# A hybrid decoder layer: wide moving operands and plain float32 in the small products

## The chip, the core and the metric

The kernel runs on one core of a Trainium2 chip. The metric is the device time of one launch in microseconds (us). Five engines work side by side, each through its own instructions in order: TensorE (PE, with its weight loads as PEld), VectorE (DVE), ScalarE (ACT), GpSimd (POOL) and SyncE (SP), which here only issues DMA transfers. Semaphores tell one engine that another has finished. The median of three runs before the change is 497.67 us (496.89 to 497.83).

## What is computed

The input x has 256 tokens of 1024 features. One product with `w_in` gives ten groups of 1024 columns: A_X and A_G (recurrent branch and its gate), S_U and S_V (spatial branch), Q, K and V (attention), G_A, G_S and G_M (a merge gate for each branch). Cut to its core, the reference is:

```python
a_x, a_gate, s_u, s_v, q, k, v, g_a, g_s, g_m = split(x @ w_in)
y_a = rg_lru(causal_dwconv(a_x, conv_w, conv_b), w_r, b_r, w_i, b_i, lam) * gelu(a_gate)
y_s = gelu(s_u) * (tril(w_s[g]) @ layer_norm(gelu(s_v)) + b_s)   # per group g, chunks of 128 tokens
y_m = moba_attention(q, k, v)          # 8 heads of 128; 256 tokens are one causal block
merged = sigmoid(g_a) * y_a + sigmoid(g_s) * y_s + sigmoid(g_m) * y_m
x1 = layer_norm(alpha * x + merged @ w_out)
h_gate, h_up = split(x1 @ w_up)        # 3072 columns each
out = layer_norm(alpha * x1 + (gelu(causal_dwconv(h_gate)) * h_up) @ w_down)
```

`rg_lru` has two block-diagonal gates, r and i (eight blocks of 128 x 128 each), and a scan over the tokens.

## The kernel before

**Three passes.** A large product is made of float32r operands: each operand is split into a rounded part, hi, and the rest, lo, and the products hi·hi, hi·lo and lo·hi are summed (`passes`). ScalarE copies a block into hi, and VectorE subtracts hi from it into lo (`split`, L64 to L66). This holds for weights and for activations.

**Chunks.** The weights come in 80 chunks of 128 x 2048 (1 MB). Forty belong to `w_in` (four of 256 columns for each group, with all eight k-tiles), four to `w_out`, 36 to the feed-forward part. `load` brings a chunk as two DMAs into two raw buffers of 1024 columns (five such buffers), `prep` splits each half. Chunks 1 to 3 come in pieces of 512, chunk 0 in eight pieces that hold a k-tile of x and one of the weights (256 columns each, 256 KB). The hi and lo parts have four buffers each, so chunk n + 4 takes the place of chunk n and can be split only when the products with chunk n are done. Loads run three chunks ahead (`LOOK`).

**Two layouts.** Feature-major (`fm_pe`, L213): the weights are stationary, the 256 tokens move, the result has features on the partitions. Token-major (`tm_mm`, L230): the activations are stationary, 256 weight columns move, the result has tokens on the partitions. S_V and V are token-major before, the other eight groups feature-major. Either way a chunk is 48 matmuls of 256 moving columns. `w_out` and `w_down` (`row_mm`, L621 to L630) move 512 columns, 24 matmuls to a chunk.

**Small products.** The mixers (`mix_step`, L367) are plain float32, 128 moving columns. The r and i gates (`ri_step`, L406), the scores of the second query tile (`score_step`, L508) and most of attention times v (`pv_step`, L562) are three-pass products of 256 columns, for which xc, `wrg`, q, k, v and the probabilities are split too. Transposes (L542, L668) are matmuls with an identity.

**The merge.** `gs_step` takes a quarter of the features at a time: sigmoid, product with the spatial branch, two sums, split into mgh and mgl. `wo0_step(c)` needs the quarter c of them.

**Order.** The program is a list of steps. TensorE's instructions stand as the list has them. The other engines' order is made by a scheduler when the kernel is built, except in the layer norm region behind `wo0_step` and in the last steps, where they keep to the list. Each engine runs its row strictly in order. Result banks are two sets of four, psa for projections, psb for the small products; a step must wait until the bank that it takes over has been read. The end of the list up to the first layer norm is q and k, scores, transposes and attention, with the projections G_A and G_S between them to cover the softmax.

Of the kernel before, what the change touches and what calls it, by code (L numbers as in the profile page):

```python
# [46 lines left out]
def trunk_kernel(ctx: ExitStack, tc, xw, x, w_in, wrg, wsT, w_out, w_up, w_down, rows, packed, out):  # L47
# [32 lines left out]
    def load(i):  # L80
        """A chunk in two halves, or, for the first chunks, in parts the arithmetic needn't wait long for"""
        parts = loaded[i] = []
        if i == 0:
            # k-tiles of the activations and of the chunk side by side
            pair = [U(f"xw{h}", (P, 4, 2, S)) for h in range(2)]
            for k in range(KT):
                t = pair[k // 4][:, k % 4 : k % 4 + 1]
                nc.sync.dma_start(t, xw[:, k : k + 1])
                parts.append((t, slice(k * S, (k + 1) * S), slice(k, k + 1)))
            return  # L90
        raw = [raws.tile([P, 1024], F32, name=f"raw{i}{h}", tag="raw") for h in range(2)]
# [992 lines left out]
```

## Time and profile before

| what | value |
|---|---|
| median of the runs (three) | 497.67 us |
| span of the profiled execution, first to last instruction | 495.1 us |
| TensorE busy | 485.0 us (98%) |
| VectorE busy | 337.7 us (68%) |
| ScalarE busy | 271.6 us (55%) |
| moved by DMA | 92.95 MB, 188 GB/s |
| granted TensorE clock, mean | 0.997 |

The span leaves out what the launch needs around the first and last instruction, so it stands 2.6 us under the median; the page gives no time of its own for the profiled execution. A matmul's duration in the trace holds its way through the array, and the next one starts long before it ends: durations of 283 ns stand 120 ns apart. What a stream of matmuls costs is therefore read from start to start. A number in brackets behind a timeline row is the time for which the engine stood before it, with what it waited for.

### The profile page before, as it was taken

The numbers are of one execution on the slowest core, as the hardware profiler recorded it, in microseconds if no ns is written. First come the engines' busy times: TensorE is split into PE (matmuls) and PEld (weight loads), VectorE is DVE, ScalarE is ACT, GpSimd is POOL, SyncE is SP. The second block draws the span as 40 slices with busy tenths as digits, with TensorE's granted clock in tenths as the row PEclk, the third lists the DMA queues.
The fourth block names the chain that finished last, engine by engine and source line by source line (L and its number), as shares of the span: only waits on it lengthen the run. The fifth ranks groups of instructions, "written<-read, shape, count | busy, mean of one in ns | idle before, by whom it ended". The sixth has DMA issues, their size and how long they took to land.

```text
span 495.1 us, 9096 instructions
## 1 busy us (share of the span) xinstructions
PE 485.0 (98%) x3728; PEld 469.7 (95%) x3728; DVE 337.7 (68%) x527; ACT 271.6 (55%) x410; POOL 21.7 (4%) x24
## 2 busy tenths in 40 slices
PE   8999999999999999999999999999999999999993
PEld 7999999999999999999998999999999999999983
DVE  5889896454449978766685987765666556666635
ACT  6746754465489288567451477645544454444431
POOL 1020000000000000000000800000000000000003
PEclk9999999999999999999999999999999999999998
DMA  8996866474523396674452448776555556555002
GB/s 288 341 372 212 283 210 219 129 228 154 169 86 128 114 317 204 206 267 137 162 170 86 133 149 280 246 252 195 190 174 191 184 184 206 171 175 178 31 1 85
DMA packets 27385, 92.95 MB, mean 188 GB/s; under 512 B 3152, under 2 KB 3536, under 8 KB 27344
## 3 DMA queue, kind: packets, MB, share of 16 engines
q1 hardware_dynamic: 27344, 92.37, 55.8%
q8 instruction: 29, 0.48, 0.4%
q14 instruction: 12, 0.10, 0.1%
HBM read 91.31 MB, written 1.05 MB: 187 GB/s over the span
## 4 chain that ended last, share of the span: by engine, by line
issue 47%; PE 41%; DVE 3%; ACT 1%; POOL 1%; ACTq 0%; DVEq 0%; POOLq 0%
PE p_u L223 14%; PE p_d L628 12%; PE p_g L223 12%; PE p_tg L237 2%; PE p_dq L628 1%; POOL rs_sv L195 1%; ACT hi L65 1%; DVE lo L66 0%; DVE va L200 0%; DVE st_m L187 0%; DVE x1Tl L66 0%; POOL rs_m L195 0%; DVE x L676 0%; PE p_x1t L668 0%; PE p_g L802 0%
## 5 line engine op out<-in xcount | busy, mean ns | idle before, releaser
L66 DVE TENSOR_TENSOR lo<-raw,hi 128x1024 fp32r<-128x1024 f32 (+1 forms) x162 | 189.0, 1193 | 81.3 <-ACT hi L65 80.6
L65 ACT CAST hi<-raw 128x1024 fp32r<-128x1024 f32 (+1 forms) x164 | 160.3, 1015 | 111.2 <-PE p_g L223 28.3
L628 PE MATMUL p_d<-hi,act 128*128 128x512 f32 x180 | 55.7, 391 | 0.0
L628 PEld LDWEIGHTS p_d<-hi,act 128*128 128x128 f32 x180 | 33.1, 188 | 6.3
L628 PE MATMUL p_d<-lo,act 128*128 128x512 f32 x90 | 35.0, 389 | 0.0
L319 DVE SCALAR_TENSOR_TENSOR cv<-p_g,par,cv 128x255 f32<-128x255 f32 (+1 forms) x48 | 23.1, 480 | 7.1 <-ACT cv L317 6.3
L223 PE MATMUL p_u<-x1Th,hi 128*128 128x256 f32 x192 | 27.0, 283 | 0.0
L223 PE MATMUL p_u<-x1Th,lo 128*128 128x256 f32 x192 | 27.0, 283 | 0.0
L223 PE MATMUL p_u<-x1Tl,hi 128*128 128x256 f32 x192 | 26.9, 283 | 0.0
L223 PEld LDWEIGHTS p_u<-x1Th,hi 128*128 128x128 f32 x192 | 25.3, 191 | 0.8
L223 PEld LDWEIGHTS p_u<-x1Th,lo 128*128 128x128 f32 x192 | 24.8, 192 | 0.0
L223 PEld LDWEIGHTS p_u<-x1Tl,hi 128*128 128x128 f32 x192 | 24.8, 192 | 0.0
L317 ACT ACTIVATE cv<-p_g,par 128x256 f32<-128x256 f32 x24 | 13.5, 563 | 19.8 <-DVE cv L319 19.8
L760 DVE TENSOR_TENSOR cv<-cv,p_u 128x512 f32<-128x512 f32 x12 | 8.2, 686 | 22.1 <-PE p_u L223 22.1
L223 PE MATMUL p_g<-x1Th,hi 128*128 128x256 f32 x160 | 22.5, 283 | 0.0
L223 PE MATMUL p_g<-x1Tl,hi 128*128 128x256 f32 x160 | 22.5, 283 | 0.0
L223 PE MATMUL p_g<-x1Th,lo 128*128 128x256 f32 x160 | 22.5, 283 | 0.0
L223 PEld LDWEIGHTS p_g<-x1Th,hi 128*128 128x128 f32 x160 | 20.6, 192 | 0.0
L223 PEld LDWEIGHTS p_g<-x1Tl,hi 128*128 128x128 f32 x160 | 20.6, 192 | 0.0
L223 PEld LDWEIGHTS p_g<-x1Th,lo 128*128 128x128 f32 x160 | 20.6, 192 | 0.0
L628 PEld LDWEIGHTS p_d<-lo,act 128*128 128x128 f32 x90 | 16.9, 188 | 3.6
L744 ACT ACTIVATE cv<-cv 128x512 f32<-128x512 f32 x12 | 7.6, 632 | 11.3 <-DVE cv L319 11.3
(241 smaller groups left out, 981.7 us busy)
## 6 DMA issues: line engine op xcount, KB each, us to landing
raw<-in_w_in SPq DMA_DIRECT2D x72, 512.0 KB, 5.1
raw<-in_w_up SPq DMA_DIRECT2D x48, 512.0 KB, 4.5
raw<-in_w_down SPq DMA_DIRECT2D x24, 512.0 KB, 4.7
raw<-in_w_out SPq DMA_DIRECT2D x8, 512.0 KB, 4.0
raw<-in_w_in SPq DMA_DIRECT2D x12, 256.0 KB, 5.4
xw<-in_xw SPq DMA_DIRECT2D x8, 256.0 KB, 4.9
gb<-in_rows SPq DMA_DIRECT2D x2, 512.0 KB, 8.1
rg_raw<-in_wrg SPq DMA_DIRECT2D x2, 512.0 KB, 6.5
```

What stands on the lines that cost most here:

```text
L65: nc.scalar.copy(hi, src)
L66: sub.tensor_sub(lo, src, hi.bitcast(F32))
L195: nc.gpsimd.tensor_tensor(rs, ve, half, op=ALU.pow)
L223: nc.tensor.matmul(dst[:, j, :], w[:, k, j * P : (j + 1) * P], a[:, k, :], start=(n == 0), stop=(n == 3 * KT - 1))
L237: nc.tensor.matmul(dst, a[:, k, tok * P : (tok + 1) * P], w[:, k, :], start=(m == 0 and k == 0), stop=(m == 2 and k == KT - 1))
L317: nc.scalar.activation(dst, src, AF.Identity, bias=pcol(bname, f), scale=w(taps - 1))
L319: nc.vector.scalar_tensor_tensor(dst[:, d:], src[:, : S - d], w(taps - 1 - d), dst[:, d:], op0=ALU.mult, op1=ALU.add)
L628: nc.tensor.matmul(dst, a[:, k0 + k, tok * P : (tok + 1) * P], w[:, k, s], start=(start and n == 0), stop=(stop and n == 6 * len(parts) - 1))
L744: nc.scalar.activation(t, t, AF.Gelu_apprx_tanh)
L760: nc.vector.tensor_mul(t, t, pf["u", c])
```

## The change

Seven of the ten input groups (`WIDE`) become token-major with 512 weight columns moving; a chunk is then 512 columns of four k-tiles, and two chunks make a half group (`wide_step`). A_X, Q and K stay feature-major (`TALL`). The first eight loads hold 256 columns of x and 512 of weights (384 KB). The raw buffers are three of 2048 columns, and from chunk 4 on a chunk is split by one ScalarE and one VectorE instruction of 2048 columns. The r and i gates, all scores, attention times v and the mixers are plain float32, and the splits for them are gone. The mixers' results and the gated branches are now token-major; `gate_step` and `merge_step` turn them into features with 32 transposes. G_A moves up beside the r and i gates, and the halves of G_S stand between the attention steps. In the names of tiles, p_w is a wide step's bank, p_ag and p_z those of the transposes.

```diff
+WIDE = (S_V, S_U, A_G, G_A, G_M, V_, G_S)
+TALL = (A_X, Q_, K_)
...
-    raws = ctx.enter_context(tc.tile_pool(name="raws", bufs=5))
+    raws = ctx.enter_context(tc.tile_pool(name="raws", bufs=3))
...
-    up = ctx.enter_context(tc.tile_pool(name="up", bufs=10))
+    up = ctx.enter_context(tc.tile_pool(name="up", bufs=9))
...
+        if i in (0, 1):
+            for k in range(4 * i, 4 * i + 4):
+                if k % 2 == 0:
+                    pair = U(f"xw{k}", (P, 2, 768))
+                t = pair[:, k % 2, :]
+                nc.sync.dma_start(t, xw[:, k, :])
+                parts.append((t, k))
             return
-        raw = [raws.tile([P, 1024], F32, name=f"raw{i}{h}", tag="raw") for h in range(2)]
+        raw = raws.tile([P, 2048], F32, name=f"raw{i}", tag="raw")
         w = 512 if i < 4 else 1024
         for at in range(0, 2048, w):
-            r = raw[at // 1024][:, at % 1024 : at % 1024 + w]
-            nc.sync.dma_start(r, chunks[i][:, at : at + w])
-            parts.append((r, slice(at, at + w), None))
+            s = slice(at, at + w)
+            nc.sync.dma_start(raw[:, s], chunks[i][:, s])
+            if w == 512:
+                parts.append((raw[:, s], s))
+        if w == 1024:
+            parts.append((raw, slice(0, 2048)))
...
+        for r, s in loaded.pop(i):
+            if i > 1:
                 split(r, hi[:, s], lo[:, s], subs.get(i, nc.vector))
                 continue
-            h, l = (t[:, s].rearrange("p (k m) -> p k m", m=S) for t in (hi, lo))
-            (nc.vector.tensor_copy if k.start == 0 else nc.scalar.copy)(h, r[:, :, 1, :])
-            split(r[:, :, 0, :], xh[:, k, :], xl[:, k, :])
-            nc.vector.tensor_sub(l, r[:, :, 1, :], h.bitcast(F32))
+            k = s
+            h, l = (t[:, (k % 4) * 512 : (k % 4 + 1) * 512] for t in (hi, lo))
+            w = r[:, 256:]
+            (nc.vector.tensor_copy if k == 0 else nc.scalar.copy)(h, w)
+            split(r[:, :256], xh[:, k, :], xl[:, k, :])
+            nc.vector.tensor_sub(l, w, h.bitcast(F32))
...
+    def wide_mm(i, dst, tok, kh, ks, ms=(0, 1, 2)):
+        hi, lo = (t.rearrange("p (k m) -> p k m", k=4) for t in ready[i])
+        pairs = passes(hi, lo, xh, xl)
+        for k in ks:
+            for m in ms:
+                w, a = pairs[m]
+                at = 4 * kh + k
+                nc.tensor.matmul(dst, a[:, at, tok * P : (tok + 1) * P], w[:, k, :],
+                                 start=(m == 0 and at == 0), stop=(m == 2 and at == KT - 1))
+    def wide_step(group, nh, use, khs=(0, 1)):
+        for kh in khs:
+            i = chunk(w_wide[4 * WIDE.index(group) + 2 * nh + kh])
+            def pe(i=i, kh=kh):
+                if kh == 0:
+                    cur["w"] = [psa.tile([P, 512], F32, name=f"p_w{group}{nh}{tok}", tag="ps") for tok in range(2)]
+                if group == S_V and nh == 0:
+                    for k in range(5):
+                        for ks, ms in (((k,), (0,)), ((k - 1,), (1, 2))):
+                            for tok in range(2):
+                                if 0 <= ks[0] < 4:
+                                    wide_mm(i, cur["w"][tok], tok, kh, ks, ms)
+                    return
+                for tok in range(2):
+                    wide_mm(i, cur["w"][tok], tok, kh, range(4))
+            def post():
+                for tok in range(2):
+                    use(tok, nh, cur["w"][tok])
+            step(pe, [i], post if kh else None)
...
     def load_rg():
...
+        rg["f"] = raw = U("rg", (P, 2, KT, P))
+        nc.sync.dma_start(raw.rearrange("p m g j -> p (m g j)"), wrg)
...
+        def pe():
+            cur["pm"] = p = psb.tile([P, 2, 2, P], F32, name=f"p_mix{c}", tag="ps")
             for j in range(2):
...
+                nc.tensor.matmul(p[:, j], ws["f"][:, g, :], va[:, :, g * P : (g + 1) * P], start=True, stop=True)
...
+            for j in range(2):
+                g = 2 * c + j
+                y = gu["f"][:, :, g * P : (g + 1) * P]
+                nc.vector.scalar_tensor_tensor(y, p[:, j], pcol("bs", g), y, op0=ALU.add, op1=ALU.mult)
...
+    def ga_use(tok, nh, p):
+        t = tmp.tile([P, 512], F32, name=f"sga{tok}{nh}", tag="t0")
+        nc.scalar.activation(t, p, AF.Sigmoid)
+        y = ag["f"][:, tok, HALVES[nh]]
+        nc.vector.tensor_mul(y, y, t)
...
             for m in range(2):
-                ops = passes(rg["h"], rg["l"], xc["h"], xc["l"])
-                for n, (w, a) in enumerate(ops):
-                    nc.tensor.matmul(p[:, m, :], w[:, m, g, :], a[:, g, :], start=(n == 0), stop=(n == 2))
+                nc.tensor.matmul(p[:, m, :], rg["f"][:, m, g, :], xc["f"][:, g, :], start=True, stop=True)
...
+            t = tmp.tile([P, 2, S], F32, name=f"i{g}", tag="t0")[:, 0, :]
+            nc.scalar.activation(t, p[:, 1, :], AF.Sigmoid, bias=pcol("bi", g))
+            nc.vector.tensor_mul(xc["f"][:, g, :], xc["f"][:, g, :], t)
...
+        hs["f"] = sq = U("sq")
...
-            nc.vector.tensor_mul(ga["f"][:, g, :], ga["f"][:, g, :], sq[:, g, :])
...
+            qk[which, c] = t = tmp.tile([P, 2, S], F32, name=f"{which}f{c}", tag=f"{which}f")
+            nc.scalar.copy(t, cur["p"])
...
                 cur["s"].append(p)
-                (qh, ql, qf), (kh, kl, kf) = qk["q", c], qk["k", c]
-                nc.tensor.matmul(p[:, :P], qf[:, j, :], kf[:, j, :], start=True, stop=True)
-                ops = passes(kh, kl, qh, ql)
-                for m, (k, q) in enumerate(ops):
-                    nc.tensor.matmul(p[:, P:], q[:, j, P:], k[:, j, :], start=(m == 0), stop=(m == 2))
+                q, k = qk["q", c], qk["k", c]
+                nc.tensor.matmul(p[:, :P], q[:, j, :P], k[:, j, :P], start=True, stop=True)
+                nc.tensor.matmul(p[:, P:], q[:, j, P:], k[:, j, :], start=True, stop=True)
...
         def post():
-            pT = U(f"pT{c}", (P, 2, 2, S), F32R)
...
-            for j in range(2):
-                split(cur["t"][j][:, :S], pT[:, 0, j, :], pT[:, 1, j, :])
-                nc.scalar.copy(last[:, j, :], cur["t"][j][:, S:])
-            probT[c] = (pT[:, 0], pT[:, 1], last)
+            probT[c] = pT = tmp.tile([P, 2, 384], F32, name=f"pT{c}", tag="pT")
+            for j in range(2):
+                nc.scalar.copy(pT[:, j, :], cur["t"][j])
...
                 s = slice((2 * c + j) * HD, (2 * c + j + 1) * HD)
-                th, tl, last = probT[c]
-                for m, (v, t) in enumerate(passes(av["h"], av["l"], th, tl)):
-                    nc.tensor.matmul(p[:, j, :], v[:, 0, s], t[:, j, :], start=(m == 0), stop=False)
-                nc.tensor.matmul(p[:, j, P:], av["r"][:, s], last[:, j, :], start=False, stop=True)
-        def post():
-            s = slice(2 * c, 2 * c + 2)
-            nc.vector.tensor_mul(sgm["f"][:, s, :], cur["o"], sgm["f"][:, s, :])
+                o = slice(j * HD, (j + 1) * HD)
+                t, v = probT[c][:, j, :], av["f"]
+                nc.tensor.matmul(p[:, 0, o], t[:, :P], v[:, 0, s], start=True, stop=True)
+                nc.tensor.matmul(p[:, 1, o], t[:, P : 2 * P], v[:, 0, s], start=True, stop=False)
+                nc.tensor.matmul(p[:, 1, o], t[:, 2 * P :], v[:, 1, s], start=False, stop=True)
+        def post():
+            y = sgm["f"][:, :, c * S : (c + 1) * S]
+            nc.vector.tensor_mul(y, cur["o"], y)
...
+    def to_features(c, y, name):
+        p = psb.tile([P, 2, S], F32, name=f"p_{name}{c}", tag="ps")
+        for k in range(2):
+            f = 2 * c + k
+            for tok in range(2):
+                nc.tensor.transpose(p[:, k, tok * P : (tok + 1) * P], y[:, tok, f * P : (f + 1) * P], ident)
+        return p
+    def gate_step(c):
+        def pe():
+            cur["pw"] = to_features(c, ag["f"], "ag")
+        def post():
+            y = hs["f"][:, 2 * c : 2 * c + 2, :]
+            nc.vector.tensor_mul(y, y, cur["pw"])
+        step(pe, [], post)
...
+    def gs_use(tok, nh, p):
+        s = HALVES[nh]
+        t = tmp.tile([P, 512], F32, name=f"sgs{tok}{nh}", tag="t0")
+        nc.scalar.activation(t, p, AF.Sigmoid)
+        y = gu["f"][:, tok, s]
+        nc.vector.tensor_mul(y, y, t)
+        nc.vector.tensor_add(y, y, sgm["f"][:, tok, s])
+    def merge_step(c):
+        def pe():
+            cur["pz"] = to_features(c, gu["f"], "z")
...
             s = slice(2 * c, 2 * c + 2)
...
+            y = hs["f"][:, s, :]
+            nc.vector.tensor_add(y, y, cur["pz"])
+            split(y, mg["h"][:, s, :], mg["l"][:, s, :])
+        step(pe, [], post)
...
+    for nh in range(2):
+        wide_step(S_V, nh, sv_use)
+    post_only(load_ws)
     for c in range(4):
-        sv_step(c)
...
+        ax_step(c)
     post_only(load_rg)
-    ax_step(2)
...
-    su_step(0)
-    su_step(1)
+    wide_step(S_U, 0, su_use)
     mix_step(0)
-    su_step(2)
     mix_step(1)
-    su_step(3)
+    wide_step(S_U, 1, su_use)
+    wide_step(A_G, 0, ag_use)
     mix_step(2)
-    ag_step(0)
     mix_step(3)
-    for c in range(1, 4):
-        ag_step(c)
-    gm_step(0)
+    wide_step(A_G, 1, ag_use)
+    for g in range(4):
+        ri_step(g)
+    wide_step(G_A, 0, ga_use)
+    for g in range(4, 8):
+        ri_step(g)
+    wide_step(G_A, 1, ga_use)
     post_only(softplus)
-    for c in range(4):
-        ri_step(2 * c)
-        ri_step(2 * c + 1)
-        if c < 3:
-            gm_step(c + 1)
-    v_step(0)
+    wide_step(G_M, 0, gm_use)
+    wide_step(G_M, 1, gm_use)
     post_only(recur)
-    for c in range(1, 4):
-        v_step(c)
+    wide_step(V_, 0, v_use)
+    wide_step(V_, 1, v_use)
     qk_step("q", 0)
     qk_step("k", 0)
+    for c in range(4):
+        gate_step(c)
     qk_step("q", 1)
     qk_step("k", 1)
     score_step(0)
     score_step(2)
     trans_step(1)
     post_only(load_mix_rows)
-    ga_step(0)
-    ga_step(1)
+    wide_step(G_S, 0, gs_use, (0,))
     pv_step(1)
     score_step(3)
     trans_step(2)
-    ga_step(2)
-    ga_step(3)
+    wide_step(G_S, 0, gs_use, (1,))
     pv_step(2)
     trans_step(3)
-    gs_step(0)
+    wide_step(G_S, 1, gs_use, (0,))
     pv_step(3)
+    merge_step(0)
+    merge_step(1)
+    wide_step(G_S, 1, gs_use, (1,))
+    wo0_step(0)
+    merge_step(2)
+    merge_step(3)
     for c in range(1, 4):
-        gs_step(c)
-    for c in range(4):
         wo0_step(c)
```

TensorE at the end of the merge, before: the last chunk of G_S (gs3) is followed by the first blocks of the output projection (p_wo; the number behind hi is the buffer, hi40 is the first chunk of `w_out`).

```order
L223 MATMUL p_gs3_3144<-xh_84,hi39_2928 128x256 x8
L223 MATMUL p_gs3_3144<-xl_85,hi39_2928 128x256 x8
L223 MATMUL p_gs3_3144<-xh_84,lo39_2929 128x256 x8
L628 MATMUL p_wo00_3210<-hi40_3006,mgh_2983 128x512
L628 MATMUL p_wo00_3210<-hi40_3006,mgl_2984 128x512
...
L628 MATMUL p_wo00_3210<-hi41_3072,mgh_2983 128x512
L628 MATMUL p_wo00_3210<-hi41_3072,mgl_2984 128x512
```

The same place after. p_w811 is the last wide bank of G_S, gu the spatial branch with the attention branch added.

```order
L534 MATMUL p_z0_2215<-ident_87,gu_697 128x128 x4
L534 MATMUL p_z1_2225<-ident_87,gu_697 128x128 x4
L255 MATMUL p_w810_2181<-hi39_2044,xh_84 128x512
...
L255 MATMUL p_w811_2182<-lo39_2045,xh_84 128x512
L592 MATMUL p_wo00_2279<-hi40_2119,mgh_2220 128x512
...
L592 MATMUL p_wo01_2280<-lo40_2120,mgh_2220 128x512
L534 MATMUL p_z2_2293<-ident_87,gu_697 128x128 x4
L534 MATMUL p_z3_2301<-ident_87,gu_697 128x128 x4
L592 MATMUL p_wo00_2279<-hi41_2177,mgh_2220 128x512
```

Behind the last G_S chunk stands one block of the output projection, then eight transposes of gu, then the other three blocks.

ScalarE there, before: copies of weight chunks (hi) and the gates' sigmoids (sgs).

```order
L65 CAST mgh_2983<-sgs2_3127 128x512
L65 CAST hi43_3204<-raw430_3200 128x1024
L601 ACTIVATE sgs3_3193<-p_gs3_3144 128x512
L65 CAST hi43_3204<-raw431_3201 128x1024
L65 CAST mgh_2983<-sgs3_3193 128x512
```

And after:

```order
L68 CAST hi42_2236<-raw42_2233 128x2048
L68 CAST mgh_2220<-sq_1290 128x512 x2
L553 ACTIVATE sgs01_2264<-p_w810_2181 128x512
L68 CAST hi43_2275<-raw43_2272 128x2048
L553 ACTIVATE sgs11_2268<-p_w811_2182 128x512
L68 CAST mgh_2220<-sq_1290 128x512 x2
```

The second token tile's sigmoid (sgs11) now stands behind the copy of the whole chunk 43, where there was half of it ahead of the last sigmoid.

VectorE there, after: rest of chunk 43 (lo43), then the product and the sum for sgs11, then what reads the transposes.

```order
L69 TENSOR_TENSOR lo42_2237<-raw42_2233,hi42_2236 128x2048
L69 TENSOR_TENSOR mgl_2221<-sq_1290,mgh_2220 128x512 x2
L555 TENSOR_TENSOR gu_697<-gu_697,sgs01_2264 128x512
L556 TENSOR_TENSOR gu_697<-gu_697,sgm_1204 128x512
L69 TENSOR_TENSOR lo43_2276<-raw43_2272,hi43_2275 128x2048
L555 TENSOR_TENSOR gu_697<-gu_697,sgs11_2268 128x512
L556 TENSOR_TENSOR gu_697<-gu_697,sgm_1204 128x512
L568 TENSOR_TENSOR sq_1290<-sq_1290,p_z2_2293 128x512
L568 TENSOR_TENSOR sq_1290<-sq_1290,p_z3_2301 128x512
L69 TENSOR_TENSOR mgl_2221<-sq_1290,mgh_2220 128x512 x2
```

The subtraction of chunk 43 stands ahead of the last product and sum, which the transposes p_z2 read.

## Rows read from the trace of the kernel before

**Rows 1.** The page: busy us (share of the span) and instructions of each engine
```profile
PE 485.0 (98%) x3728; PEld 469.7 (95%) x3728; DVE 337.7 (68%) x527; ACT 271.6 (55%) x410; POOL 21.7 (4%) x24
```

**Rows 2.** Waits of TensorE: who waits, for whom; us in total, times, longest
```profile
PE p_sv L237 <- ACT xh L65: 1.0, 3, 0.5
PE p_x1t L668 <- DVE x L718: 0.6, 1, 0.6
```

**Rows 3.** The chain of waits: start us, us, what; two blocks of the feed-forward part
```profile
306.63 5.76 PE p_g L223 x48
312.39 5.47 PE p_d L628 x24
```

**Rows 4.** Timeline of TensorE at the gates: start, us, instruction, out<-in, operand sizes
```profile
107.85 0.28 PE L406 MATMUL p_ri<-xch,rg_hi 128*128 128x256 f32 x1
...
109.29 0.52 PE L223 MATMUL p_gm<-xh,hi 128*128 128x256 f32 x3
```

**Rows 5.** Timeline of TensorE at a mixer, and the block behind it
```profile
63.99 1.06 PE L367 MATMUL p_mix<-ws_raw,va 128*128 128x128 f32 x8
64.80 1.20 PE L223 MATMUL p_su<-xh,hi 128*128 128x256 f32 x8
65.83 0.40 PE L223 MATMUL p_su<-xl,hi 128*128 128x256 f32 x2
```

**Rows 6.** Timeline of TensorE: a score block, then attention times v
```profile
176.97 0.39 PE L505 MATMUL p_s<-kf,qf 128*128 128x128 f32 x2
...
178.14 0.64 PE L223 MATMUL p_q<-xh,hi 128*128 128x256 f32 x4
...
202.99 0.40 PE L562 MATMUL p_o<-pT,avh 128*128 128x256 f32 x2
...
204.15 0.39 PE L505 MATMUL p_s<-kf,qf 128*128 128x128 f32 x2
```

**Rows 7.** Timeline of TensorE: eight transposes
```profile
277.06 1.09 PE L668 MATMUL p_x1t<-ident,x 128*128 128x128 f32 x8
277.90 0.36 PE L628 MATMUL p_woq<-hi,mgh 128*128 128x256 f32 x1
```

**Rows 8.** Timeline of TensorE at the start, and GB/s in the page's 40 slices
```profile
4.51 0.50 PE L237 MATMUL p_sv<-hi,xh 128*128 128x256 f32 x2
...
17.91 1.12 PE L237 MATMUL p_sv<-hi,xh 128*128 128x256 f32 x8
...
GB/s 288 341 372 212 283 210 219 129 228 154 169 86 128 114 317 204 206 267 137 162 170 86 133 149 280 246 252 195 190 174 191 184 184 206 171 175 178 31 1 85
```

**Rows 9.** Groups by shape: line, operation, count | busy us, mean ns | idle before
```profile
L66 DVE TENSOR_TENSOR lo<-raw,hi 128x1024 fp32r<-128x1024 f32 x150 | 181.5, 1233 | 81.2 <-ACT hi L65 80.6 <-PE p_wo L628 0.3
L65 ACT CAST hi<-raw 128x1024 fp32r<-128x1024 f32 x152 | 153.5, 1046 | 111.1 <-PE p_g L223 28.3 <-PE p_u L223 21.0 <-DMA raw<-in_w_in 14.1
...
L66 DVE TENSOR_TENSOR lo<-raw,hi 128x512 fp32r<-128x512 f32 x12 | 7.5, 688 | 0.1
...
L65 ACT CAST hi<-raw 128x512 fp32r<-128x512 f32 x12 | 6.7, 626 | 0.1
```

**Rows 10.** Timeline of ScalarE and of VectorE at the last gate group
```profile
258.64 0.58 ACT L601 ACTIVATE sgs<-p_gs 128x512 f32<-128x512 f32 x1
...
261.65 0.68 DVE L603 TENSOR_TENSOR sgs<-sgs,ga 128x512 f32<-128x512 f32 x1
262.36 0.69 DVE L604 TENSOR_TENSOR sgs<-sgs,sgm 128x512 f32<-128x512 f32 x1
```

**Rows 11.** Stretch 18:62: its length, busy (instructions) by engine, clock, DMA share, GB/s
```profile
18.00:62.00 44.00, 44.00 (x369) 44.00 (x368) 38.82 (x57) 28.67 (x40) 4.02 (x3) 1.00 0.83 292
```

**Rows 12.** Stretches of the tail; the column behind POOL is the granted clock
```profile
487.00:488.00 1.00, 0.56 (x5) 0.36 (x3) 0.40 (x1) 0.00 (x0) 0.70 (x1) 1.00 0.00 0
488.00:492.00 4.00, 0.00 (x0) 0.00 (x0) 3.78 (x11) 1.39 (x3) 0.00 (x0) 1.00 0.48 191
493.00:494.00 1.00, 0.00 (x0) 0.00 (x0) 0.00 (x0) 0.00 (x0) 0.00 (x0) 0.50 0.43 144
```

More of the change, by code (lines that the diff above doesn't have):

```diff
@@ L46, in trunk_kernel @@
 @with_exitstack
-def trunk_kernel(ctx: ExitStack, tc, xw, x, w_in, wrg, wsT, w_out, w_up, w_down, rows, packed, out):
+def trunk_kernel(ctx: ExitStack, tc, xw, x, w_wide, w_tall, wrg, wsT, w_out, w_up, w_down, rows, packed, out):
     nc = tc.nc
@@ L238, in tm_mm @@
                                  start=(m == 0 and k == 0), stop=(m == 2 and k == KT - 1))
-    def tm_pe(c, dst):
-        for tok in range(2):
-            tm_mm(c, dst[:, tok, :], tok, range(KT), (xh, xl))
+    def wide_mm(i, dst, tok, kh, ks, ms=(0, 1, 2)):
[26 more added lines that the diff above has]
+            step(pe, [i], post if kh else None)
     cur = {"acts": (xh, xl)}
@@ L297, in load_ws @@
         ws["f"] = raw
-        bs = U("bs", (P, D))
-        load_row(bs, 2)
-        ws["b"] = bs
     rg = {}
     def load_rg():
-        hi = U("rg_hi", (P, 2, KT, P), F32R)
-        lo = U("rg_lo", (P, 2, KT, P), F32R)
-        for m in range(2):
-            raw = raws.tile([P, KT, P], F32, name=f"rg_raw{m}", tag="raw")
-            nc.sync.dma_start(raw.rearrange("p g j -> p (g j)"), wrg[:, m * D : (m + 1) * D])
-            split(raw, hi[:, m], lo[:, m])
-        rg["h"], rg["l"] = hi, lo
+        rg["f"] = raw = U("rg", (P, 2, KT, P))
+        nc.sync.dma_start(raw.rearrange("p m g j -> p (m g j)"), wrg)
     def conv(dst, src, wname, bname, f, stride, taps):
@@ L360, in mix_step @@
     def mix_step(c):
         def pe():
-            p = psb.tile([P, 2, 2, P], F32, name=f"p_mix{c}", tag="ps")
-            cur["pm"] = p
+            cur["pm"] = p = psb.tile([P, 2, 2, P], F32, name=f"p_mix{c}", tag="ps")
             for j in range(2):
                 g = 2 * c + j
-                for n in range(2):
-                    nc.tensor.matmul(p[:, j, n, :], va[:, n, g * P : (g + 1) * P], ws["f"][:, g, :],
-                                     start=True, stop=True)
+                nc.tensor.matmul(p[:, j], ws["f"][:, g, :], va[:, :, g * P : (g + 1) * P], start=True, stop=True)
@@ L370, in post @@
         def post():
             p = cur["pm"]
-            g = slice(2 * c * P, (2 * c + 2) * P)
-            b = ws["b"][:, g].rearrange("p (j t) -> p j t", j=2)
-            t = tmp.tile([P, 2, 2, P], F32, name=f"mix{c}", tag="t0")
-            for n in range(2):
-                nc.vector.tensor_add(t[:, :, n, :], p[:, :, n, :], b)
-            ys = gu["f"][:, 2 * c : 2 * c + 2, :]
-            nc.vector.tensor_mul(ys, ys, t.rearrange("p j n t -> p j (n t)"))
-        step(pe, [], post)
-    ga = {}
@@ L484, in post @@
         def post():
-            if which == "q":
-                qk[c] = U(f"qk{c}", (P, 4, 2, S), F32R)
-            o = 0 if which == "q" else 2
-            hl = (qk[c][:, o], qk[c][:, o + 1])
-            split(cur["p"], *hl)
-            first = tmp.tile([P, 2, P], F32, name=f"{which}f{c}", tag=f"{which}f")
-            nc.scalar.copy(first, cur["p"][:, :, :P])
-            qk[which, c] = (*hl, first)
+            qk[which, c] = t = tmp.tile([P, 2, S], F32, name=f"{which}f{c}", tag=f"{which}f")
+            nc.scalar.copy(t, cur["p"])
         step(pe, [i], post)
@@ L1056, with group, quarters @@
     pack = {"cw": a["conv_rg_w"][0], "cb": a["conv_rg_b"], "br": a["b_rgate"], "bi": a["b_igate"],
-            "lam": a["lru_lambda"], "fw": a["conv_ffn_w"][0], "fb": a["conv_ffn_b"]}
+            "lam": a["lru_lambda"], "fw": a["conv_ffn_w"][0], "fb": a["conv_ffn_b"],
+            "bs": a["b_spatial"][0]}
     xT = x.T.reshape(KT, P, S).transpose(1, 0, 2)
-    w_in = cols(a["w_in"][0])
+    w = a["w_in"][0]
+    def group(g):
+        return w[:, g * D : (g + 1) * D]
+    def quarters(w):
+        return w.reshape(2, 4, P, 2, 512).transpose(3, 0, 2, 1, 4).reshape(4, P, 2048)
+    first = group(S_V)[:, :512].reshape(KT, P, 512).transpose(1, 0, 2)
     arrays = {
-        "xw": cont(np.stack([xT, w_in[4 * S_V].reshape(P, KT, S)], axis=2)),
+        "xw": cont(np.concatenate([xT, first], axis=2)),
         "x": cont(x),
-        "w_in": w_in,
+        "w_wide": cont(np.concatenate([quarters(group(g)) for g in WIDE])),
+        "w_tall": cont(np.concatenate([cols(group(g)) for g in TALL])),
         "wrg": cont(np.stack([a["w_rgate"][0], a["w_igate"][0]]).transpose(2, 0, 1, 3)).reshape(P, 2048),
```

172 lines of the change are left out of this document (43 added, 129 removed).

## The prediction

> **What bounds the kernel now.** I read the busy times first. TensorE is at work for 485.0 of 495.1 us, VectorE for 337.7, ScalarE for 271.6 [rows 1]. The waits on TensorE's queue come next, and there are hardly any: 1.0 us for the first loads and 0.6 us at the second layer norm [rows 2]. What is left of its 10 us without work is the start and the tail. The chain of waits then shows nothing but blocks of matmuls over its last 200 us, two of which are [rows 3]. So the time is the sum of TensorE's instructions, and the change must be added up there; VectorE and ScalarE count only where TensorE comes to wait for them, which before it does nowhere in the mixers.
>
> **The wide products.** One weight chunk is 48 matmuls of 256 moving columns before and 24 of 512 after. The trace has both for equal work: 48 of 256 take 5.76 us, 24 of 512 take 5.47 [rows 3]. Seven groups of four chunks are 28 chunks, and 28 x 0.29 is 8.1. The 5.47 holds a change of width at its end; wide steps mostly follow each other, which adds a little, so I take -8.5 (-8.0 to -9.0).
> The Trainium skill (page "TensorE: Matmul & The Clock Gate", section "Back-to-back issue gap") gives the spacing of isolated matmuls at the full clock as columns / 2.4 plus 2.5 ns. By it a chunk would be 5.24 us narrow and 5.18 wide, the saving of 28 chunks 1.7 us in place of 8.5, and the forecast below some 505. The rows (120 and 228 ns a matmul) differ and decide.
>
> **The small products.** A mixer step of before is four plain float32 products of 128 columns, two records each in the trace. It takes 0.81 us to the next block, whose first eight matmuls take 1.03 instead of 8 x 0.12 = 0.96: 0.88 in all, 0.22 each [rows 5]. The trace has none of 256 columns. Twice the columns took 1.9 times as long in the three-pass products (0.228 against 0.120), and one of 256 columns can't take less than one of 128. The floor is thus 0.22, the ceiling 0.44; the nearest row with a factor of 1.9 to 2 gives 0.43.
> Recurrence gates: 48 three-pass matmuls, twelve in 1.44 us [rows 4], are 5.76; 16 x 0.43 is 6.9: +1.1. Scores: a block is 1.17 us before [rows 6]; now 2 x (0.22 + 0.43) = 1.30: +0.5 for four. Attention times v: 1.16 before [rows 6], now 6 x 0.22 = 1.32: +0.65 for four. Mixers: sixteen of 128 columns (3.5 us) become eight of 256 (3.4): nothing. At the floor of 0.22 gates, scores and mixers would give 7 us back; nothing in the rows speaks for that.
>
> **The transposes.** 32 are new: 16 of the gated branch behind the first q and k, 16 in the merge. Eight took 0.84 us [rows 7], and a switch back costs 0.07, as behind the mixers [rows 5]. 32 x 0.105 and three switches come to +3.6 (3.3 to 3.9).
> TensorE's own work thus changes by -8.5 + 1.1 + 0.5 + 0.65 + 3.6 = -2.65.
>
> **The start.** The first eight loads carry 384 KB, not 256. TensorE starts at 4.51 and has the first two chunks' work done at 17.91: 13.4 us for 11.5 of work [rows 8]. The loads move up to 341 GB/s there [rows 8], so 256 KB in 0.77 us and 384 KB in 1.15. The larger first piece comes some 0.7 us later (0.38 more, twice, since a second piece shares the transfer), but to each piece there is 1.36 us of work where there was 0.72, so that the loads, which were a little too slow, now keep ahead. I expect the half group done at 16.9; 0.5 of that gain stands in the wide term already: -0.5 (-0.9 to +0.5).
>
> **The merge: a new wait.** Before, the third gate group's last sigmoid, sums and splits had three blocks of the output projection (8.2 us) in front of them. After, only one block lies between the last wide step (its end is E) and the transposes p_z2, whose second one reads the second token tile. Weight chunk 43 takes the buffers of chunk 39, which is in use until E. ScalarE's order has the copy of chunk 43, now one of 2048 columns, ahead of the sigmoid; VectorE's has its subtraction ahead of the product and sum that follow the sigmoid. A copy of 512 takes 0.63 and of 1024 1.05, so 2048 about 1.89; subtractions 0.69 and 1.23, so 2.32 [rows 9]. The sigmoid (0.58) hides beside the subtraction; product and sum take 0.71 and 0.69 [rows 10]. E + 1.89 + 2.32 + 1.40 and 0.1 of hand-over is E + 5.7. TensorE has 12 x 0.228 and a transpose, so stands from E + 2.85: +2.85. If the long instructions took no longer than those of 1024, the wait is 0.95; if twice as long, 3.2. Queued behind it are the other transposes and all that follows; the last sums and splits of the merge then have a 2.7 us block in front of them, and the first pair of them needs some 2.1.
>
> **Small waits.** p_t11 takes the bank of p_t10 and so waits for ScalarE's copy out of it. ScalarE is ready in time: from the end of k3 it copies chunk 39 and k3 (1.89 + 0.63), while TensorE has 1.32 + 1.30 + 0.32 of work. But the copy itself, some 0.5, has nothing in front of it: +0.55 (0 to 0.7). The second token tile of the first u step needs a bank that VectorE frees after its convolutions; it is busy 38.8 of 44 us there [rows 11], and loses 5.2 us of splits (four of 512, two of 1024 columns [rows 9]), so +0.4 (0 to 1.3) for this and the first down block together. Fewer, longer raw buffers cost nothing: a chunk of 1 MB needs 3.1 us at 341 GB/s, its copy and subtraction 4.2; with three buffers that is 2.4 us a chunk, and some 3 with the delay of a load, against 5.5 of TensorE work. The final layer norm and the feed-forward part stay as they are.
>
> **Sum.** -2.65 - 0.5 + 2.85 + 0.55 + 0.4 = +0.65. The profiled execution's span of 495.1 lies 2.6 under the median of 497.67; its other overhead should stay. 497.67 + 0.65 is 498.3.
>
> **Rivals.** First, the merge wait is mostly absent, since the long split instructions run faster than their shorter kin suggest, or the work behind the sigmoid is sooner done; the wait is then under 1 us and the time 496.4, with the small waits gone too 495.4. A float32 product of 256 columns at 0.33, halfway to the floor, gives the same 495.1 (32 of them, 3.2 less) from another side. For it: TensorE waits almost nowhere before. Against: both orders put the whole chunk first, and the buffers aren't free earlier.
> Second, slower: TensorE's clock falls at that wait. The granted clock stands at 1.00 wherever TensorE works; after its last matmul (487.6) it stays 1.00 to 492, and reads 0.50 later [rows 12], which is 1.2 GHz. A stand of 2.85 us is shorter than that one, but transposes and a second short block lie behind it. If it falls, the twelve matmuls of the next block at half speed add 2.7: 501.0, from the point where the level drops at all.
> The Trainium skill (same page, section "Part 4: PE-mode transpose") says that transposes do not count as TensorE activity for that gate, which would make a fall likelier here; no run yet shows it.
> Third, slower too: VectorE comes late with a whole split of 2048 in the convolutions (before the u steps) or the softmax, where halves could be slipped between. One instruction late is +2.3: 500.6. For it: 88% busy there [rows 11]. Against: 5 us of splits leave that stretch.
> Fourth, a wide block is as slow as two narrow ones, the change does not do what it says: 498.3 + 8.5 = 506.8; against it the down and output projections, which run so [rows 3].
>
> **How the numbers follow.** Forecast 0.45, own range 497.0 to 499.6; merge wait absent or cheaper float32 0.28; clock 0.11; late splits 0.14; the fourth 0.02. About 0.2% (1.0 us) is what can be told from no change here: faster is under 496.7, slower over 498.7. The forecast gives 0.05, 0.24 and 0.16; the first rival 0.24 faster and 0.04 same; the rest is slower, but for 0.02. Together 0.29 faster, 0.30 same, 0.41 slower. The range, 495.0 to 501.2, takes in the first three rivals.
>
> **What would show it.** Right: a chunk of wide projection at about 5.45 us; TensorE's waits led by p_z2 on VectorE's sum with gu, near 2.8; p_t11 waiting half a microsecond for ScalarE; 16 gate products at 0.43. Wrong: no wait at p_z2, a granted clock of 0.5 behind it, waits of any wide step for a split, or a first half group that ends after 18.

## The result and the profile after

The changed kernel takes 502.63 us (median of four runs, 501.74 to 503.14) against 497.50 before (496.89 to 497.83): a ratio of 1.0102, 95% interval 1.0088 to 1.0116. It is slower by 5.1 us, and lies above the predicted range. The profiled execution has a span of 501.3, 6.2 more than before. One run below, the profiled one of number 1, was in a slower state (689.54 us at a mean clock of 0.657) and is left out of the figures.

The page's busy line answers to [rows 1]: the other engines were relieved as planned, but TensorE is busy for 2.0 us more, not 2.65 less.

```profile
PE 487.0 (97%) x3056; PEld 438.3 (87%) x3056; DVE 314.1 (63%) x410; ACT 258.2 (52%) x302; POOL 23.0 (5%) x23
```

TensorE's waits, beside [rows 2] (us in total, times, longest):

```profile
PE p_z L534 <- DVE gu L556: 2.6, 1, 2.6
PE p_x1t L632 <- POOL x L219: 1.0, 1, 1.0
...
PE p_t L501 <- ACT pT L507: 0.6, 1, 0.6
...
PE p_w L255 <- DVE xc L330: 0.5, 1, 0.5
```

The wait at the merge (p_z on gu) is there, and so is that of p_t11. The last row stands at 54.62 us: the second token tile of the first u step, for a bank that VectorE's convolutions free.

The chain of waits, beside [rows 3] (start, us, what):

```profile
100.30 3.45 PE p_ri L394 x16
...
118.40 56.00 PE p_w L255 x240
174.40 5.68 PE p_q L232 x48
...
185.76 1.75 PE p_ag L534 x16
...
312.68 5.76 PE p_g L232 x48
318.44 5.47 PE p_d L592 x24
```

240 wide matmuls without a gap take 56.00 us: 0.2333 each, 5.60 a chunk. The down products, of the same shape, still take 5.47 a chunk, 0.228 each. So the wide projections do run like single instructions of 512 columns, but 2.4% slower than those from which the prediction took their price. The narrow q block takes 5.68, less than the 5.76 of p_g, which has the same shape too.

TensorE's timeline (start, us, instruction, out<-in, operands), beside [rows 4 to 8]: the end of the first half group, a score block, attention times v, and the merge.

```profile
17.25 0.40 PE L255 MATMUL p_w<-hi,xh 128*128 128x512 f32 x1
...
211.38 0.38 PE L466 MATMUL p_s<-kf,qf 128*128 128x128 f32 x2
...
212.69 0.82 PE L501 MATMUL p_t<-ident,prob 128*128 128x128 f32 x6
...
224.72 0.38 PE L518 MATMUL p_o<-av,pT 128*128 128x128 f32 x2
...
226.05 0.39 PE L466 MATMUL p_s<-kf,qf 128*128 128x128 f32 x2
...
261.44 0.27 PE L534 MATMUL p_z<-ident,gu 128*128 128x128 f32 x1
264.30 1.75 PE L534 MATMUL p_z<-ident,gu 128*128 128x128 f32 x7 [2.59 <-DVE gu L556]
265.70 0.78 PE L592 MATMUL p_wo<-hi,mgh 128*128 128x512 f32 x1
266.27 0.63 PE L592 MATMUL p_wo<-hi,mgl 128*128 128x512 f32 x1
266.70 0.60 PE L592 MATMUL p_wo<-lo,mgh 128*128 128x512 f32 x1
267.13 0.40 PE L592 MATMUL p_wo<-hi,mgh 128*128 128x512 f32 x1
```

The score block is 1.31 us long, attention times v 1.33, sixteen transposes (above) 1.75, a gate product 3.45/8 = 0.431 for two records: all within 0.02 of their predicted prices. At the merge TensorE stands 2.59 us, and then the seven transposes take 1.40 from start to start (seven of [rows 7] take 0.74) and the first output products behind them 0.57 and then 0.43 apiece: half speed. The stretches show it (length, busy us and instructions of PE, PEld, DVE, ACT, POOL, granted clock, DMA share, GB/s):

```profile
263.00:264.00 1.00, 0.00 (x0) 0.00 (x0) 0.96 (x2) 0.00 (x0) 0.00 (x0) 0.86 0.04 8
264.00:265.00 1.00, 0.70 (x4) 0.70 (x5) 0.24 (x1) 0.00 (x0) 0.00 (x0) 0.50 0.83 258
...
267.00:268.00 1.00, 1.00 (x5) 0.77 (x5) 0.92 (x2) 0.43 (x1) 0.00 (x0) 0.93 0.36 135
```

The clock goes to 0.50 (1.2 GHz) within the stand and comes back at 267. The mean of 0.86 in 263 to 264, where TensorE does nothing, says that it fell near 263.7, before the seven transposes began at 264.30: they can't be what lowered it. The row of work that ends the stand, on ScalarE and then on VectorE, beside [rows 10]:

```profile
258.68 1.91 ACT L68 CAST hi<-raw 128x2048 fp32r<-128x2048 f32 x1 [1.91 <-PE p_w L255]
```
```profile
260.62 2.29 DVE L69 TENSOR_TENSOR lo<-raw,hi 128x2048 fp32r<-128x2048 f32 x1 [1.56 <-ACT hi L68]
262.83 0.68 DVE L555 TENSOR_TENSOR gu<-gu,sgs 128x512 f32<-128x512 f32 x1
263.55 0.69 DVE L556 TENSOR_TENSOR gu<-gu,sgm 128x512 f32<-128x512 f32 x1
```

It is the predicted one: copy, subtraction, product, sum, each within 0.03 of its estimate.

### The profile page after: what moved, and what is told of

Same layout as the page of the kernel before. It is cut to its first block, busy times and chain, and to the rows that moved or that the text cites. A ratio compares the mean times of both kernels' runs of the same rounds, so it can differ in the third digit from the quotient of the medians.

```text
span 501.3 us, 7464 instructions
## 1 busy us (share of the span) xinstructions
PE 487.0 (97%) x3056; PEld 438.3 (87%) x3056; DVE 314.1 (63%) x410; ACT 258.2 (52%) x302; POOL 23.0 (5%) x23
## 4 chain that ended last, share of the span: by engine, by line
PE 89%; DVE 4%; DMA 2%; ACT 2%; POOL 1%; issue 1%; SPq 0%; ACTq 0%; DVEq 0%; POOLq 0%
PE p_w L255 30%; PE p_u L232 14%; PE p_d L592 12%; PE p_g L232 11%; PE p_q L232 5%; PE p_k L232 5%; PE p_wo L592 3%; PE p_tg L244 2%; DVE lo L69 2%; PE p_ri L394 1%; ACT hi L68 1%; DMA raw<-in_w_wide 1%; PE p_dq L592 1%; DMA xw<-in_xw 1%; PE p_s L467 1%
## 5 line engine op out<-in xcount | busy, mean ns | idle before, releaser
L69 DVE TENSOR_TENSOR lo<-raw,hi 128x2048 fp32r<-128x2048 f32 (+1 forms) x83 | 176.7, 2135 | 102.1 <-ACT hi L68 97.3
L68 ACT CAST hi<-raw 128x2048 fp32r<-128x2048 f32 (+1 forms) x84 | 149.4, 1784 | 127.3 <-PE p_w L255 34.6
L255 PE MATMUL p_w<-hi,xh 128*128 128x512 f32 x224 | 88.4, 401 | 1.7 <-ACT xh L68 0.7
L255 PE MATMUL p_w<-hi,xl 128*128 128x512 f32 x224 | 88.5, 395 | 0.0
L255 PE MATMUL p_w<-lo,xh 128*128 128x512 f32 x224 | 88.4, 395 | 0.0
L255 PEld LDWEIGHTS p_w<-hi,xh 128*128 128x128 f32 x224 | 41.9, 188 | 12.5 <-ACT xh L68 1.8
L255 PEld LDWEIGHTS p_w<-lo,xh 128*128 128x128 f32 x224 | 42.0, 187 | 10.2
L255 PEld LDWEIGHTS p_w<-hi,xl 128*128 128x128 f32 x224 | 42.0, 188 | 9.9
```

Source lines behind the costliest of these rows:

```text
L68: nc.scalar.copy(hi, src)
L69: sub.tensor_sub(lo, src, hi.bitcast(F32))
L255: nc.tensor.matmul(dst, a[:, at, tok * P : (tok + 1) * P], w[:, k, :], start=(m == 0 and at == 0), stop=(m == 2 and at == KT - 1))
```

## The experiments

**The theories.** First: 5.60 against 5.47 comes from where the operands lie. In the built program the constants (`par`, bs among them) are 8 columns wider after, and the raw buffers are other ones; the weight buffers thus start at byte 60320 of a partition instead of 56192, while x stays at 16512. What I call distance is the start of the moving operand less that of the stationary one, modulo 256 bytes. It is 0 in every projection of before; after, 32 with the weights moving and 224 with x moving. The feed-forward activations moved along with the weights, and their blocks did not change (5.76, 5.47). Rival: the wide form itself is slow here, by its DMA traffic or by the width. Second: the standing TensorE drops the clock. Rival: the transposes do, or the next block is late by itself. The seven transposes behind the stand are ruled out by the stretches above.

**1. Weight buffers 32 bytes on, in after.**

```diff
-    par = const.tile([P, NPACK], F32, name="par")
+    par = const.tile([P, NPACK + 8], F32, name="par")
```

> Only the parameter tile is 32 bytes longer, so that the weight buffers start on a multiple of 64 bytes again, like x's own buffers; instructions and order are the same. Theory A (place): a wide matmul took 0.233 us instead of 0.227 because the weights lie 32 bytes off the line on which x lies, and the 256-column chunks with x took 5.68 instead of 5.76 for the same reason. Then a wide chunk takes 5.45 here, a chunk of A_X, Q or K 5.76, and the time falls by 28 x 0.15 - 12 x 0.08 = 3.2 us to about 499.4. Theory B (form): 0.233 is what 512 columns cost with x stationary; then nothing changes, 502.6.

Measured: 499.44 (median of nine runs, 499.00 to 501.02), ratio to before 1.0053 (1.0037 to 1.0069): some 3 us of the 5.1 are gone with an edit that changes no instruction. The spacing is read from number 5, and there the total proves to be right by luck: a wide chunk takes 5.50, not 5.45, and a block of q 5.46, not 5.76. So a line of 64 bytes is not the rule. Theory A2 in what follows is the distance modulo 256, as defined above.

**2. The same 32 bytes in before.**

```diff
-    par = const.tile([P, NPACK], F32, name="par")
+    par = const.tile([P, NPACK + 8], F32, name="par")
```

> The kernel before, with the parameter tile 32 bytes longer, so that its weight buffers lie 32 bytes off x's. Theory A (place): its 32 feature-major chunks of the input projection take 5.68 in place of 5.76, the feed-forward part stays, since its activations move by 32 bytes too: about 2.6 us less, 494.9; the 8 token-major chunks of 256 columns are open. Theory B: the place does nothing, 497.5.

Measured: 493.73, ratio 0.9925 (0.9901 to 0.9949). Timeline of TensorE, from the first v block to the end of the first q block:

```profile
129.66 1.10 PE L237 MATMUL p_v<-hi,xh 128*128 128x256 f32 x8
...
152.07 1.11 PE L223 MATMUL p_q<-xh,hi 128*128 128x256 f32 x8
...
157.75 0.52 PE L223 MATMUL p_k<-xh,hi 128*128 128x256 f32 x3
```

Four token-major chunks take 22.41 us (5.60 each) and the feature-major one 5.68, where before had 5.76. The distance of 32 that slows 512 columns speeds up 256. So the old price of a narrow block belonged to its place too, and the comparison in [rows 3] was of two shapes at one distance, 0.

**3. The ordered region from one step earlier**, so that the sigmoids of the last gate group stand ahead of the copy of chunk 43.

```diff
+    early = len(steps)
...
-        if n in (ordered[0], ordered[2]):
+        if n in (early, ordered[2]):
```

> The region in which ScalarE and VectorE keep to the list begins one step sooner, so the last sigmoid, product and sum of the merge stand ahead of the copy and subtraction of chunk 43. Theory: the 2.6 us wait at p_z2 came from that order and goes; a wait of up to 0.5 us at the third block of the output projection comes in its place. If the fall of the granted clock came from the wait, it goes too (1.5 us): together -3.7 us, 498.9. If the clock fell because of the transposes, it still falls: -2.2, 500.4. If the wait is not due to the order, no change.

Measured: 499.38, ratio 1.0042 (1.0029 to 1.0055), 3.2 less than after. TensorE's waits no longer have p_z; what is left of the merge is this:

```profile
PE p_wo L592 <- DVE mgl L69: 0.2, 1, 0.2
```

The stretch that holds most of its eight transposes p_z, which take from 261.31 to 262.10, shows full clock, as does the next one up to 266 (columns as above):

```profile
258.00:262.00 4.00, 4.00 (x23) 3.34 (x22) 3.01 (x5) 2.40 (x2) 0.00 (x0) 1.00 0.70 237
```

The wait is a matter of the row's order, and eight transposes without a stand left the clock at 1.00 in this execution.

**4. The wait filled:** 25 bf16 matmuls of 128 columns, unused, ahead of the transposes p_z2.

```diff
+    def filler():
+        def pe():
+            ones = nc.const_aps.tensor(1.0, [P, P], mybir.dt.bfloat16)
+            p = psa.tile([P, 512], F32, name="p_fill", tag="ps")
+            for _ in range(FILL):
+                nc.tensor.matmul(p[:, :P], ones, ones, start=True, stop=True)
```

> 25 small bfloat16 matmuls (0.1 us each, results unused) stand ahead of p_z2, so that TensorE is at work during the wait of 2.6 us. Theory: the wait remains, but the granted clock stays at 1.00, and the output projection behind it runs at 0.227 a matmul: -1.5 us, 501.1. Rival: the clock falls because of the transposes, and nothing changes; 502.6.

Measured: 502.87, ratio 1.0111 (1.0080 to 1.0142). The place itself, by TensorE's timeline:

```profile
262.57 1.64 PE L877 MATMUL p_fill<-const-bfloat16-1.0 128*128 128x128 bf16 x25
...
265.44 0.98 PE L535 MATMUL p_z<-ident,gu 128*128 128x128 f32 x7 [1.11 <-DVE gu L557]
266.18 0.48 PE L593 MATMUL p_wo<-hi,mgh 128*128 128x512 f32 x1
```

Seven transposes in 0.74 and full speed behind them; from the first output block to the transposes p_x1t 22.75 us in place of 24.12, the 1.4 that was expected. The total does not show it: this execution lost 1.1 us at its start, where matmuls stood 0.43 apart until 8.8 us, as after's did at a clock of 0.50, far ahead of the edit. The total is inconclusive. The place says that the late data alone do not cost the 1.4; that the filling kept the clock up is not shown by it, since number 9 keeps the clock with the same stand unfilled.

**5. Numbers 1 and 3 together.**

```diff
+    par = const.tile([P, NPACK + 8], F32, name="par")
...
+        if n in (early, ordered[2]):
```

> Both edits at once: the weight buffers on the line of 64 bytes, and the sigmoid ahead of chunk 43. If the two causes are apart, their gains add: wide chunks of 5.45 us, chunks of A_X, Q and K of 5.76, no wait at p_z2, granted clock 1.00 there; 502.6 - 2.6 - 3.2 = 496.8, and so 0.1 to 0.2% under the kernel before. If they share a cause (a slower TensorE makes the wait), less than the sum: 498.

Measured: 495.49, ratio 0.9962 (0.9947 to 0.9977). With both repaired, the changed kernel beats before by 0.4%, and the expectation by 1.3 us. The chain:

```profile
119.14 54.95 PE p_w L255 x240
174.10 5.46 PE p_q L232 x48
...
306.98 5.76 PE p_g L232 x48
```

Wide 0.2290 at distance 64, q 5.46 at distance 192 (the last q and k blocks 5.66 and 5.65), and the feed-forward block, at distance 0 still, 5.76.

**6 and 7. Other distances for the narrow products:** the weight buffers 2064 columns wide, narrow chunks 8 columns in; number 6 on top of 5, number 7 in before.

```diff
+        o = 8 if i in off else 0
+        hi = his.tile([P, 2064], F32R, name=f"hi{i}", tag="hi")[:, o : o + 2048]
+        lo = los.tile([P, 2064], F32R, name=f"lo{i}", tag="lo")[:, o : o + 2048]
```

> As the last, and the weights of A_X, Q, K and of the up projection, whose matmuls have 256 columns, stand 32 bytes off the line inside their buffers, while the wide and the 512-column ones stay on it. Theory A (place): a 256-column matmul is cheaper off the line (0.1183 against 0.120), a 512-column one on it (0.227 against 0.233); 34 feature-major chunks save 0.08 each and the first two gate chunks 0.16: -3.0, about 493.8. If it was not the place of weights and activations to each other but something else that moved with the tile, nothing changes.

> The kernel before, with the weights of the input and up projections 32 bytes off inside their buffers, nothing else moved. Theory A: 54 feature-major chunks save 0.08 each, the ten token-major ones of 256 columns 0.15 each (5.60 for 5.76, as V's took with the longer parameter tile): 4.3 + 1.5 = 5.8 us, 491.5. Rival (the gain of the longer parameter tile came from elsewhere, raw buffers or x): nothing, 497.3.

Measured: number 6 497.47, ratio 1.0010 (0.9997 to 1.0023), a miss by 3.7; number 7 492.91, ratio 0.9915 (0.9897 to 0.9933), 1.4 over what was expected. Chain of number 6, then two feed-forward blocks of number 6 and the same two of number 7:

```profile
117.62 55.50 PE p_w L257 x240
173.12 5.63 PE p_q L234 x48
178.75 5.68 PE p_k L234 x48
186.17 5.61 PE p_q L234 x48
191.78 5.76 PE p_k L234 x48
...
335.59 5.61 PE p_u L234 x48
341.19 5.75 PE p_g L234 x48
```
```profile
332.48 5.61 PE p_u L225 x48
338.09 5.75 PE p_g L225 x48
```

I had overlooked that buffers of 8256 bytes put the four of a pool at four distances, 64 apart, in both. Blocks now go 5.61 to 5.76 by the buffer they got, and the wide ones rise to 0.2313. The four q and k blocks shown lie at 160, 224, 32 and 96. In number 7 the same four got the buffers at 224, 32, 96 and 160, and TensorE's timeline has them 5.68, 5.61, 5.75 and 5.64 long. The feed-forward blocks shown lie at 32 and 96 in both, while the weights' own addresses differ by 64 bytes modulo 256 between the two kernels. The miss thus speaks for the theory more than a hit would have: the time follows the distance, and not the address.

**8. Splits of 1024 again**, the long raw buffers kept.

```diff
-            if w == 512:
-                parts.append((raw[:, s], s))
-        if w == 1024:
-            parts.append((raw, slice(0, 2048)))
+            parts.append((raw[:, s], s))
```

> The changed kernel with a chunk split in two instructions of 1024 columns on each engine, as before; the raw buffers stay three of 2048. The sigmoid then stands between the two copies of chunk 43, product and sum on either side of the second subtraction: the sum ends at about E + 4.8, where E is the end of the last wide step, and the wait at p_z2 is 2.0 instead of 2.6. If the fall of the clock needs the longer wait, it goes (1.5 us); the first rival to the order (the long instructions as such) would have the wait under 1. 502.6 - 0.6 to - 2.1: 500.5 to 502.0.

Measured: 499.43, ratio 1.0041 (1.0013 to 1.0069), 1 us better than expected. TensorE's waits:

```profile
PE p_z L531 <- DVE gu L553: 1.7, 1, 1.7
...
PE p_x1t L629 <- DVE x L679: 0.6, 1, 0.6
```

The halves take 0.9 off the first wait, 0.3 off the second (0.97 to 0.64) and 0.3 off that of p_t11, and the wait for the convolutions' bank, 0.5, is gone. The granted clock of this execution stays at 1.00 behind the stand of 1.7 us, which spares what the fall cost in after, 1.35. That is 3.35 of the 3.6 us by which its span is shorter.

**9. Distance 0, as before, in after** (224 bytes more).

```diff
+    par = const.tile([P, NPACK + 56], F32, name="par")
```

> Only the parameter tile is longer (224 bytes), so that the moving and the stationary operand of every large product lie at the same distance from a line of 256 bytes, as they do in the kernel before. Theory A2 (places to each other, modulo 256 bytes): wide chunks then take 5.45 us (0.227 a matmul) as predicted, chunks of A_X, Q and K 5.76: 502.6 - 4.2 + 1.0 = 499.4. Theory A (modulo 64, as in the first run on this) gives the same as with 32 bytes: 5.51 and 5.47 a chunk, 500.0. Theory B (form): 5.60 and 502.6.

Measured: 498.60 (498.15 to 501.70), ratio 1.0053 (1.0027 to 1.0080). Chain, timeline and stretches:

```profile
116.30 54.41 PE p_w L255 x240
170.71 5.75 PE p_q L232 x48
```
```profile
260.74 0.98 PE L534 MATMUL p_z<-ident,gu 128*128 128x128 f32 x7 [2.60 <-DVE gu L556]
261.48 0.47 PE L592 MATMUL p_wo<-hi,mgh 128*128 128x512 f32 x1
```
```profile
261.00:263.00 2.00, 2.00 (x14) 1.74 (x13) 1.58 (x3) 0.95 (x2) 0.00 (x0) 1.00 0.86 301
```

A wide chunk is 5.44 and a narrow one 5.75: the prices of [rows 3] return with the distance of [rows 3], and the wide form as such is not slow. The wait is 2.60, as in after, and the clock stays: the fall comes in some executions and not in others. The mean clock of the runs fits: after has 0.991 at 503.1 us twice, 0.995 at 501.7 and 502.2; number 9 has 0.991 and 0.988 at 500.1 and 501.7, and 0.995 or 0.996 at 498.2 to 498.6. It doesn't say where the clock fell, though: the profiled execution of number 5 has 0.992 for a clock of 0.50 from 6.9 to 10.3 us, at its start.

**10. Before with every projection and every u and gate block at distance 192.**

```diff
+        o = off.get(i, 0)
+        hi = his.tile([P, 2112], F32R, name=f"hi{i}", tag="hi")[:, o : o + 2048]
+        lo = los.tile([P, 2112], F32R, name=f"lo{i}", tag="lo")[:, o : o + 2048]
...
+        off[i] = 48 if group in (S_V, V_) else 16
```

> The kernel before, no width changed: only the weight buffers are 256 bytes longer, and a chunk of the input and up projections lies in them so that its matmuls' moving operand stands 192 bytes (modulo 256) behind the next stationary one. Theory A2: feature-major matmuls of 256 columns take 0.114 us in place of 0.120, as A_X, Q and K did where they lay so: 54 chunks save 0.28 each, 15.1 us, and the ten token-major chunks something between 0 and 0.28: 480 to 482. Rival (0.114 came from the other layout of that kernel): no change, 497.5.

Measured: 488.66, ratio 0.9830 (0.9811 to 0.9849): the fastest version here, though 7 to 9 us short of what was expected. Its chain:

```profile
296.01 5.46 PE p_u L225 x48
...
312.37 5.65 PE p_u L225 x48
```

Blocks of one shape at one distance have two lengths, about 5.45 and 5.65, each for several blocks in a row. Why is open.

**11. After with number 3 and the best distances** (0 for 512 columns, 192 for 256).

```diff
+    par = const.tile([P, NPACK + 56], F32, name="par")
...
+        off[i] = 16
...
+        if n in (early, ordered[2]):
```

> The changed kernel with all that was found: sigmoid ahead of chunk 43, wide and 512-column products at distance 0, those of 256 columns at 192. Theory A2: against the run with both edits (495.5) wide chunks go from 5.51 to 5.45 (-1.7), 22 up chunks from 5.76 to 5.48 and two gate chunks likewise (-6.7): 487.1. It should stay behind the kernel before with the same places (480 to 482), since a wide chunk at 5.45 is then worth no more than a narrow one at 5.48, while the transposes and float32 products remain as extra work.

Measured: 493.09, ratio 0.9925 (0.9909 to 0.9941), 6 us over what was expected, for the reason left open in number 10 (5.65 in every feed-forward block of this shape, where 5.48 was expected, and 5.66 in most of q and k). It stays 4.4 us behind number 10, as expected: at these places a wide chunk (5.44) is worth no more than a narrow one at its shorter length (5.45) and 0.2 less than one at its longer, and the transposes come on top.

## Why the prediction was wrong

**The wide products: the step that failed.** The prediction said that a chunk would fall from 5.76 to 5.45 us and 28 of them give 8.5 back. They gave 28 x (5.76 - 5.60), about 4.5. The mechanism (one wide instruction for two narrow ones) was right, the size was not: I took the price from the down products, whose operands lie at distance 0, and never asked whether the new layout would put the weights elsewhere. Number 9 puts them back, measures 5.44, and lands at 498.60, within the forecast's own range, though 1.7 above its own before rather than 0.65. The same shift made A_X, Q and K cheaper: 12 x 0.08, about 1.0, also not foreseen.

**The clock, rival two.** It happened in the profiled execution: seven transposes lost 0.66, and the 72 output products behind them 0.69 (17.13 us against 16.44 in number 9), 1.35 in all, for an estimated 2.7. It was rated as another case to the forecast; it is a risk on top of it. That the stand brings it is supported, not proven: a mean clock of 0.992 or less stands in 13 of the 18 runs with the whole stand (after, numbers 1 and 9), in 3 of the 29 without it (numbers 3, 5, 6 and 11), in none of the 4 with it filled and none of the 5 with 1.7 us of it. What decides whether it falls, no run shows. The Trainium skill (page "TensorE: Matmul & The Clock Gate", section "Part 4: PE-mode transpose") says that transposes don't count as busy time for the gate in the same way. Number 3, whose eight transposes follow other work at once, and number 9, with seven behind the stand, kept the clock at 1.00, and in after it fell before the seven began, so that rule decided nothing here.

**What was right.** The merge wait: 2.85 predicted, 2.59 measured, by the named row of instructions. p_t11: 0.55 and 0.57. Float32 of 256 columns: 0.43 and 0.431. Gates +1.1, scores +0.56, attention times v +0.7, transposes +3.5 are as worked out. The small waits (0.4): 0.49, at the second token tile of the first u step, the place that was named, for VectorE's convolutions.

**Smaller misses.** The first two chunks' work is done at 17.25, not 16.9: of the 0.66 gained, 0.3 belongs to the wide term, so -0.35 for -0.5. The wait at p_x1t grew by 0.33, and this was not in the list: GpSimd's two additions took 5.10 us beside one long subtraction of VectorE, where they took 3.96 beside two short ones in before, which themselves took 4.22. In number 8, with halves, 3.96, 4.22 and the wait of before (0.64) are back. GpSimd's row of after (the subtraction of 128x2048 runs from 280.92 for 2.29):

```profile
279.24 5.10 POOL L219 TENSOR_TENSOR x<-x,gbm 128x512 f32<-128x512 f32 x2 [1.91 <-DVE x L217]
```

The terms as measured: -4.5 - 1.0 + 1.1 + 0.56 + 0.7 + 3.5 - 0.35 + 2.59 + 1.35 + 0.57 + 0.49 + 0.33 = +5.3, of the 6.2 that the span grew; 0.9 is not placed.

## What to carry to other kernels

A price per instruction read from one stage held for another here only where the operands lay alike: compare the built addresses of moving and stationary tiles before and after a change, since any tile that grows by a few columns moves all that are allocated behind it. Where TensorE is the bound, try a few offsets of its buffers first; that was worth 1.7% here with no change to the work, more than the rewrite gave at any placement tried. And where a long instruction replaces two, look for the urgent short one that now stands behind it.

## What the hardware showed that was not expected

The spacing of three-pass matmuls, start to start, by the distance defined above. x stands still in all of these; that it is the distance and not the weights' own address rests on the feed-forward blocks, which did not change when both moved, and on numbers 6 and 7.

| columns | distance | ns | from |
|---|---|---|---|
| 512 | 0 | 227 | number 9 |
| 512 | 64 | 229 | number 5 |
| 512 | 32 | 233 | after |
| 256 | 0 | 120 | before |
| 256 | 96 | 120 | numbers 6, 7 |
| 256 | 224 | 118 | after, numbers 2, 6, 7 |
| 256 | 160 | 117 to 119 | numbers 6, 7 |
| 256 | 32 | 117 | numbers 2, 6, 7 |
| 256 | 192 | 113 to 114, or 118 | numbers 5, 10, 11 |

The rule in the Trainium skill (page "TensorE: Matmul & The Clock Gate", section "Back-to-back issue gap"), columns / 2.4 plus 2.5 ns, would give 216 and 109; no run here reached either, and it has no term for the place. Why, of the distances tried, 0 is best for 512 columns and among the worst for 256, and what makes the two levels at 192, no run here shows. Within a stand of 2.6 us TensorE's clock fell to 0.50 in one profiled execution, and in another it stayed at 1.00.
